# One core, a hybrid decoder layer: another pace of products in the issue order, the output projection's products in another order, the last branch's operands and the weight sums issued at other times

## The chip, the cores and the metric

The kernel runs on one core of one Trainium2 chip. The metric is the device time of one execution in microseconds. TensorE is called PE here, VectorE DVE, ScalarE ACT, GpSimd POOL and SyncE SP; each takes its instructions strictly in the order in which the program gives them, and waits for another engine or a transfer by semaphores.

## The reference, cut to what matters

One layer of a sequence model over 512 tokens of width 1024: two token mixers side by side, merged by gates, an output projection, and a gated feed-forward part.

```python
u = rmsnorm(h, g_mix[l])
proj = u @ w_in[l]          # retention q k v gate, DeltaNet q k v z, two merge gates
ro = retention_chunkwise(rotary(rq), rotary(rk), rv)           # 8 heads
y_ret = (silu(rgate) * groupnorm(ro)) @ w_ret_br[l]
qkv = silu(causal_dwconv(concat(dq, dk_, dv_), dn_conv_w[l]))
do = gated_delta_chunkwise(l2norm(cq), l2norm(ck), cv, g, beta)  # 8 heads, chunks of 128
y_dn = (rmsnorm(do) * silu(dz)) @ w_dn_br[l]
merged = sigmoid(gate_r) * y_ret + sigmoid(gate_d) * y_dn
h = h + merged @ w_o[l]
u2 = rmsnorm(h, g_ffn[l])
a, b = split(causal_dwconv(u2 @ w_up[l], ffn_conv_w[l]) + ffn_conv_b[l])
h = h + (silu(a) * b) @ w_down[l]
```

In each chunk of the DeltaNet a triangular system of 128 rows is solved for every head and chunk. All of it is float32.

## The kernel before

**Products.** Each float32 operand is split into a high and a low part, and one product of the layer becomes three on PE: high with high, high with low, low with high (`mm3`). A weight block is fetched by SP into `wraw` (L243, L245), cast on ACT to `whi`, and `wlo` is made on DVE as `wraw - whi`; both casts are issued some blocks ahead of their use, and SP fetches the next block when one has been split. All matmuls are recorded at L176, all transpositions at L180, and every instruction of ACT, DVE and POOL at L161, the line of a helper.

**Stages, in order of time.** Normalisation and transposition of x; input projections of the first four DeltaNet heads (`pk`, `pq`, `pv`, 256 or 512 columns); then the retention projections `pr`, while DVE solves the first four heads' triangular systems; the next four heads' and the gates' projections (`pz`) with the second solve; then five square matrices of 1024 x 1024, each by seven half-size products instead of eight: two merge gates (matrices 0 and 1), the DeltaNet branch (2), the retention branch (3, all as `py`), the output projection (4, called OUT, as `po`); then the feed-forward up projection (`pa`, `pb`) and down projection (`pd`, 5, called DOWN).

**A solve.** The kernel writes the matrices A to DRAM (L753), reads them back in another layout as `sa` (L816), and substitutes on DVE in 31 steps, each one `xtmp<-sa,xx` and one `xx<-xx,xtmp`. The result goes by DRAM (`x_dram`, L829) into `tt` (L832), SP issuing these transfers between its weight fetches. The small products `pm<-tt,A` on PE then combine the 32-row blocks; the first of them needs the whole solve.

**Seven products.** `PRODUCTS` (L61) names each product's weights and operand. Sums of weight quarters (`s1` to `s4`, table `SUMS`) are made in DRAM by POOL's DMAs (`presum`, L266): four copies and then four accumulating transfers of 1024 KB for each matrix, in pieces for DOWN. `presums` spreads them over a stretch of planned time; before each one ACT writes a small `tick` and POOL reads it into `tock`, so that the DMA is issued where ACT has come to. Matrix 3's sums are spawned with the eight `pz` blocks of the DeltaNet gate, OUT's after matrix 0, DOWN's after matrix 3. The operands of matrices 2 and 3 (`d` from the DeltaNet, `r` from retention; T1 to T4 are sums of quarters) are made by `operands_c`, chained one after another in `all_operands`, each part not before a given product (`since`) has begun; `oh` and `ol` are the two parts of such an operand.

**What sets the order.** The class `Order` (L102) is a planner that runs while the program is built. It has a clock, which every PE instruction advances (`product`, 512 columns by 512/2400 = 0.2133 us, from L173), and a clock for each other engine from a cost by size (DVE: 0.08 + 0.00104 us a column, so 0.61 us for 512 and 1.14 us for 1024; ACT: 0.12 + 0.00085; POOL: 0.3 + 0.001). Dependent work is written as generators, which are resumed when the planned clock has passed the planned end of their last instruction by 0.3 us (`HOP`) or more. So the planner's prices decide between which products a transposition or a small product stands, and in which order ACT, DVE and POOL take their work. Nothing of it runs on the chip.

**Output projection.** `m_out` transposes each finished quarter of the merged branches (`pmt`, copied to `mr`), and makes the operands: `mB` from quarters, `mt` and `mT` (T1 to T4) from their differences, each split on ACT and DVE. The products stand in the order 0, 3, 2, 5, 4, 1, 6 (`OUT_ORDER`) and are added into `h1` (x, loaded by SP at L1295 ahead of matrix 3) on DVE by `o_into`; when a row block is whole its sum of squares (`ssq`, by `junk`) gives `rs`, and `hs` is the scaled row, transposed on PE (`pt<-cst,hs`) and split to `u2hi`, `u2lo` for the feed-forward part.

## Time and profile before

| what | value |
|---|---|
| median of 3 runs | 1030.83 us (1028.68 to 1032.12) |
| profiled execution | 1029.81 us, its span 1028.0 us |
| PE busy | 993.4 us (97% of the span), 5241 instructions |
| DVE busy | 733.9 us (71%) |
| ACT busy | 528.7 us (51%) |
| POOL busy | 168.9 us (16%) |
| chain that ended last | PE 76%, DVE 14%, DMA 4%, issue 3%, ACT 2% |
| mean granted clock of PE | 0.985 |
| moved by DMA | 189.29 MB, mean 184 GB/s |

PE is busy nearly all the time, so a microsecond is to be had or lost mostly where PE stands idle, or where its clock is lowered. The share of the span does not show these places: the page's table of waits, the timeline and the table by stretches do. A wait is put down to the engine or transfer that came last.

### The profile page before, as it was taken

The page shows a single profiled execution, that of the slowest core. Times are in us where ns is not written, and L with a number is a line of the kernel's source. Part 1 is how long each engine was busy: PE and PEld are TensorE (multiplying, and loading weights), DVE is VectorE, ACT ScalarE, POOL GpSimd, SP SyncE. Part 2 cuts the span into 40 slices and gives each one's busy share as a digit, 9 for nine tenths or more (in the row PEclk, how much of TensorE's full clock was granted, in tenths as well). Part 3 has the DMA queues.
Part 4 walks back from the last instruction along what each step waited for, and adds up shares of the span by engine and source line. Part 5 has one row for each costly group of instructions (what it writes and reads, how often), then busy time and mean ns, then how long its engine had stood idle before and what let it go on. Part 6 is the DMA issues. An engine that isn't in the chain of part 4 may idle for free.

```text
span 1028.0 us, 14392 instructions
## 1 busy us (share of the span) xinstructions
PE 993.4 (97%) x5241; PEld 826.0 (80%) x5241; DVE 733.9 (71%) x1370; ACT 528.7 (51%) x1120; POOL 168.9 (16%) x220
## 2 busy tenths in 40 slices
PE   8999999999999998999999998899999999999997
PEld 7888887887788876888888776698888888888886
DVE  5777897457777785556789699856555676778785
ACT  5699222475545323557676456445444433346664
POOL 3021111023323112320111001221112111000001
PEclk9999999999999998999999989989999999999999
DMA  6343457856956935478889955835589899246763
GB/s 239 104 129 126 136 202 164 188 186 148 188 195 165 203 102 173 134 159 245 277 271 283 289 181 183 315 115 196 187 181 205 183 193 204 89 123 193 205 185 122
DMA packets 82614, 189.29 MB, mean 184 GB/s; under 512 B 23088, under 2 KB 31600, under 8 KB 82544
## 3 DMA queue, kind: packets, MB, share of 16 engines
q1 hardware_dynamic: 55024, 123.36, 36.9%
q0 software_dynamic: 27520, 65.02, 28.9%
q8 instruction: 41, 0.67, 0.3%
q14 instruction: 29, 0.24, 0.1%
HBM read 185.17 MB, written 68.19 MB: 246 GB/s over the span
## 4 chain that ended last, share of the span: by engine, by line
PE 76%; DVE 14%; DMA 4%; issue 3%; ACT 2%; POOL 1%; SPq 0%; POOLq 0%; DVEq 0%
PE py L176 14%; PE pa L176 12%; PE pb L176 12%; PE pd L176 10%; DVE wlo L161 4%; PE pq L176 4%; PE pk L176 3%; PE pz L176 3%; PE pv L176 3%; PE psc L176 3%; PE pr L176 3%; DVE xtmp L161 3%; PE po L176 2%; DVE xx L161 2%; PE pm L176 2%
## 5 line engine op out<-in xcount | busy, mean ns | idle before, releaser
L161 ACT CAST whi<-wraw 128x1024 fp32r<-128x1024 f32 x212 | 219.6, 1036 | 151.6 <-PE py L176 46.3
L161 DVE TENSOR_TENSOR wlo<-wraw,whi 128x1024 fp32r<-128x1024 f32 x212 | 254.7, 1203 | 52.9 <-ACT whi L161 52.5
L161 POOL TENSOR_SCALAR tock<-tick 128x1 f32<-128x1 f32 x72 | 27.8, 387 | 533.9 <-ACT tick L161 524.9
L161 DVE SCALAR_TENSOR_TENSOR acc<-pb,prm,acc 128x511 f32<-128x511 f32 (+1 forms) x44 | 33.0, 749 | 57.2 <-ACT acc L161 56.4
L176 PE MATMUL pa<-u2lo,whi 128*128 128x512 f32 (+1 forms) x192 | 72.4, 377 | 0.7 <-DVE u2lo L161 0.7
L176 PE MATMUL pa<-u2hi,whi 128*128 128x512 f32 (+1 forms) x192 | 72.7, 379 | 0.0
L176 PE MATMUL pa<-u2hi,wlo 128*128 128x512 f32 (+1 forms) x192 | 72.2, 376 | 0.0
L176 PE MATMUL pb<-u2hi,whi 128*128 128x512 f32 (+1 forms) x184 | 69.9, 380 | 0.0
L176 PE MATMUL pb<-u2lo,whi 128*128 128x512 f32 (+1 forms) x184 | 69.9, 380 | 0.0
L176 PE MATMUL pb<-u2hi,wlo 128*128 128x512 f32 (+1 forms) x184 | 69.9, 380 | 0.0
L176 PE MATMUL py<-whi,ol 128*128 128x512 f32 x160 | 63.3, 396 | 2.8 <-DVE ol L161 2.8
L176 PE MATMUL py<-whi,oh 128*128 128x512 f32 x160 | 63.6, 398 | 1.4 <-ACT oh L161 1.4
L176 PE MATMUL py<-wlo,oh 128*128 128x512 f32 x160 | 63.0, 394 | 0.0
L176 PE MATMUL pd<-whi,T 128*128 128x512 f32 (+1 forms) x198 | 55.4, 366 | 0.0
L176 PE MATMUL pz<-uhi,whi 128*128 128x512 f32 x128 | 53.0, 414 | 0.0
L176 PE MATMUL pr<-whi,uhi 128*128 128x512 f32 x128 | 52.5, 410 | 0.0
L176 PE MATMUL pz<-ulo,whi 128*128 128x512 f32 x128 | 50.6, 395 | 0.0
L176 PE MATMUL pz<-uhi,wlo 128*128 128x512 f32 x128 | 50.6, 395 | 0.0
L176 PE MATMUL pr<-whi,ulo 128*128 128x512 f32 x128 | 50.1, 391 | 0.0
L176 PE MATMUL pr<-wlo,uhi 128*128 128x512 f32 x128 | 50.0, 390 | 0.0
L161 DVE SCALAR_TENSOR_TENSOR acc<-pa,prm,acc 128x511 f32<-128x511 f32 (+1 forms) x44 | 32.9, 749 | 19.0 <-ACT acc L161 18.2
L176 PEld LDWEIGHTS pa<-u2lo,whi 128*128 128x128 f32 x192 | 37.1, 193 | 7.2 <-DVE u2lo L161 0.9
(320 smaller groups left out, 2456.1 us busy)
## 6 DMA issues: line engine op xcount, KB each, us to landing
wraw<-w SPq DMA_DIRECT2D x100, 512.0 KB, 4.6
s<-wm POOLq DMA_DIRECT2D x30, 1024.0 KB, 6.6
wraw<-s SPq DMA_DIRECT2D x60, 512.0 KB, 4.6
s<-wd POOLq DMA_DIRECT2D x24, 704.0 KB, 5.7
wraw<-wm SPq DMA_DIRECT2D x30, 512.0 KB, 4.8
s<-s POOLq DMA_DIRECT2D x10, 1024.0 KB, 11.3
wraw<-wd SPq DMA_DIRECT2D x15, 512.0 KB, 3.7
s<-s POOLq DMA_DIRECT2D x8, 704.0 KB, 8.9
```

The costliest lines, as they stand in the source:

```text
L161: return f(out, *args, **kw)
L176: self.engine.matmul(out, lhsT, rhs, start=start, stop=stop, **kw)
```

## The change

Five things change in the program; what is computed stays the same, up to the order of additions into `h1`.

1. In the planner each split float32 product costs 0.0135 us more: 0.2268 us for 512 columns instead of 0.2133, 0.1202 us for 256 instead of 0.1067. No other price is changed.
2. The output projection's products stand in the order 0, 5, 2, 3, 4, 1, 6. Product 5 is now alone in bank E; product 3 has a bank F of its own, which `fourth` adds to both halves of `h1`, so that DVE has two additions more. The banks are allocated where they are first used.
3. In `m_out`, B22 is split as soon as it is there; for B12, T2 comes first, T1 after 2.5 us and T3 after another 2.5 us of planned time, where T1 came first, then T2, B22 and T3.
4. The `r` operands are spawned on their own instead of behind the `d` operands, and their last parts may begin one product earlier (`since` 14, 15, 16, 17 for 14, 15, 17, 18).
5. The sums of matrix 3 and of OUT are issued one after the other, eight steps over 65 us of planned time each, from the `up` of the last DeltaNet head; matrix 3's no longer begin with the `pz` blocks, nor OUT's after matrix 0.

```diff
--- before.py
+++ after.py
@@ -57,7 +57,7 @@
 
 OUT, DOWN = 4, 5
 INNER = (HK, HK, HK, HK, HK, NK)
-OUT_ORDER = (0, 3, 2, 5, 4, 1, 6)
+OUT_ORDER = (0, 5, 2, 3, 4, 1, 6)
 PRODUCTS = (("w11", "B11"), ("w12", "B21"), ("s2", "T2"), ("s1", "T1"), ("s3", "T3"), ("s4", "B22"), ("w22", "T4"))
 WD = {"w11": 0, "w12": 1, "w21": 2, "w22": 3}
 SUMS = (("s1", "w21", "w22"), ("s3", "w11", "w21"), ("s2", "w11", "s1"), ("s4", "w12", "s2"))
@@ -170,7 +170,7 @@
     def matmul(self, out, lhsT, rhs, start, stop, **kw):
         m = max(lhsT.shape[-1], out.shape[-1])
         if lhsT.dtype == F32R:
-            self.order.product(max(256, out.shape[-1]) / 2400)
+            self.order.product(0.0135 + max(256, out.shape[-1]) / 2400)
         else:
             self.order.product(max(2 * m, 4 * out.shape[-1], 64) / 2400)
         self.engine.matmul(out, lhsT, rhs, start=start, stop=stop, **kw)
@@ -251,8 +251,11 @@
 
     def quarter(s, name):
         if name not in WD:
+            assert (s, name) in made
             return sums[s, name]
         return (io["wd"] if s == DOWN else io["wm"][s])[WD[name]]
+
+    made = set()
 
     def presum(s, parts):
 
@@ -265,6 +268,8 @@
                     kw = dict(accum_op=ALU.add) if add else {}
                     nc.gpsimd.dma_start(sums[s, name][:, c], quarter(s, b if add else a)[:, c],
                                         max_dma_last_dim=2048, **kw)
+                    if add and i == parts - 1:
+                        made.add((s, name))
                     yield
 
     def pace():
@@ -1159,21 +1164,24 @@
                 spawn(parts_of(opnd, (("B21", c), ("B22", c)), raw[c + HK]))
                 combine_c(raw, x, c)
                 yield gap
-        for c in range(HK):
-            while (x, c) not in sums_of or now[0] < since[2]:
-                yield 0.5
-            spawn(parts_of(opnd, (("T2", c), ("T4", c)), sums_of[x, c][1]))
-            yield gap
-        for c in range(HK):
-            while now[0] < since[3]:
-                yield 0.5
-            spawn(parts_of(opnd, (("T3", c), ("T1", c)), sums_of[x, c][0]))
-            yield gap
+        names = ("T3", "T1"), ("T2", "T4")
+        for n, i in enumerate((1, 0)):
+            for c in range(HK):
+                while (x, c) not in sums_of or now[0] < since[2 + n]:
+                    yield 0.5
+                spawn(parts_of(opnd, [(name, c) for name in names[i]], sums_of[x, c][i]))
+                yield gap
+
+    def late_sums():
+        while "up" not in heads[H - 1]["got"]:
+            yield 0.5
+        for s in (3, OUT):
+            yield from presums((s,), 1, (order.clock, order.clock + 65.0, 8))
 
     for src, raw, x in ((roT, rr_, "r"), (doT, dd, "d")):
         if x == "d":
             spawn(u_raw(), 8.0)
-            spawn(presums((3,), 1, (order.clock + 8.0, order.clock + 70.0, 8)))
+            spawn(late_sums())
         for c in range(8):
             spawn(gate_out(dense_c(u, "pz"), c, src, raw, x))
 
@@ -1181,9 +1189,9 @@
     def all_operands():
         yield from operands_c(u_opnd, None, "u", 1.2, (0, 0, 0, 0))
         yield from operands_c(d_opnd, dd, "d", 2.0, (8, 9, 12, 13))
-        yield from operands_c(r_opnd, rr_, "r", 2.0, (14, 15, 17, 18))
 
     spawn(all_operands())
+    spawn(operands_c(r_opnd, rr_, "r", 2.0, (14, 15, 16, 17)))
     gates = [{}, {}]
     merged = {}
 
@@ -1206,21 +1214,20 @@
         m = o_raw[name, half] = S(f"mr{t}{i}")
         act.copy(m, pt)
         yield
-        if name in ("B11", "B21"):
+        if name in ("B11", "B21", "B22"):
             spawn(o_split(name, half, m))
         if name == "B12":
-            t1 = S("mt1")
-            vec.tensor_tensor(t1, o_raw["B11", half], m, ALU.subtract)
-            spawn(o_split("T1", half, t1), 0.2)
-            yield
             t3 = S("mt3")
             vec.tensor_tensor(t3, o_raw["B22", half], m, ALU.subtract)
             t2 = o_raw["T2", half] = S("mt2")
             vec.scalar_tensor_tensor(t2, t3, -1.0, o_raw["B11", half], ALU.mult, ALU.subtract)
             spawn(o_split("T2", half, t2), 0.2)
-            yield 1.5
-            spawn(o_split("B22", half, o_raw["B22", half]), 0.2)
-            spawn(o_split("T3", half, t3), 1.8)
+            yield 2.5
+            t1 = S("mt1")
+            vec.tensor_tensor(t1, o_raw["B11", half], m, ALU.subtract)
+            spawn(o_split("T1", half, t1), 0.2)
+            yield 2.5
+            spawn(o_split("T3", half, t3), 0.2)
         elif name == "B21":
             yield 1.5
             t4 = S("mt4")
@@ -1285,7 +1292,6 @@
     hold(lambda: len(normed) == H and all("o" in hd["got"] for hd in heads))
     mix.close()
     late.append(ctx.enter_context(tc.tile_pool(name="heap2", bufs=1, reuse_waits="tile")))
-    spawn(presums((OUT,), 1, (order.clock, order.clock + 75.0, 8)))
     h1 = [[None] * 2 for _ in range(NT)]
     for s, opnd in ((1, u_opnd), (2, d_opnd), (3, r_opnd)):
         if s == 3:
@@ -1333,12 +1339,22 @@
         yield from split(u2hi[k][:, ck(t)], u2lo[k][:, ck(t)], ps, prm[:, P_GF + k:P_GF + k + 1])
         u2_ready.add((t, k))
 
-    A, E, C = ([PS("po") for _ in range(2)] for _ in range(3))
+    def fourth(t, ps):
+        yield from o_into(2 + t, 1, ps, ALU.subtract)
+        yield from o_into(2 + t, 0, ps, ALU.add, True)
+
+    def bank():
+        return [PS("po") for _ in range(2)]
+
+    A = bank()
     product(0, o_get, HK, [[(full, A[t], True, o_into(t, 0, A[t], ALU.add))] for t in range(2)])
-    product(3, o_get, HK, [[(full, E[t], True, o_into(2 + t, 1, E[t], ALU.subtract))] for t in range(2)])
+    E = bank()
+    product(5, o_get, HK, [[(full, E[t], True, o_into(2 + t, 0, E[t], ALU.add))] for t in range(2)])
     product(2, o_get, HK, [[(full, A[t], False, o_into(2 + t, 0, A[t], ALU.add))] for t in range(2)])
-    product(5, o_get, HK, [[(full, E[t], False, o_into(2 + t, 0, E[t], ALU.add, True))] for t in range(2)])
+    F = bank()
+    product(3, o_get, HK, [[(full, F[t], True, fourth(t, F[t]))] for t in range(2)])
     product(4, o_get, HK, [[(full, A[t], False, o_into(2 + t, 1, A[t], ALU.subtract, True))] for t in range(2)])
+    C = bank()
     product(1, o_get, HK, [[(full, C[t], True, o_into(t, 0, C[t], ALU.add, True))] for t in range(2)])
     product(6, o_get, HK, [[(full, A[t], False, o_into(t, 1, A[t], ALU.subtract, True))] for t in range(2)], tail=2)
     u2 = (u2hi, u2lo)
```

The counts of PE, ACT and POOL instructions stay as they are; DVE has two more. Where the instructions stand is another matter. Three places follow, first before and then now.

PE, at the first small product after the first solve (`tt` is the solve's result, `pr` the retention projections, whose `uhi_154` to `uhi_161` are the eight blocks of u):

```order
L176 MATMUL pr<-whi,ulo_163 128x512
L176 MATMUL pr<-whi,uhi_156 128x512
L176 MATMUL pr<-wlo,uhi_156 128x512
L176 MATMUL pr<-whi,ulo_164 128x512
L176 MATMUL pm_1907<-tt_178,A_632 32x32 x8
L176 MATMUL pr<-whi,uhi_157 128x512
L176 MATMUL pr<-wlo,uhi_157 128x512
```

```order
L176 MATMUL pr<-whi,uhi_161 128x512
L176 MATMUL pr<-wlo,uhi_161 128x512
L176 MATMUL pr<-whi,ulo_169 128x512
L176 MATMUL pm_1858<-tt_178,A_619 32x32 x8
L176 MATMUL pr<-whi,uhi_160 128x512
L176 MATMUL pr<-wlo,uhi_160 128x512
L176 MATMUL pr<-whi,ulo_168 128x512
```

Ahead of this `pm` stood 555 products of 512 columns and 96 of 256 columns; now 522 and 96 stand there. Thirty-three `pr` products have moved behind it. At the second solve the first `pm` has moved forward too, from 1146 products of 512 columns ahead of it to 1131.

ACT, at the last `tick` that releases one of OUT's sums on POOL (`oh<-r`, `oh<-rz`, `oh<-ry` are operands of matrix 3, `oh<-dz`, `oh<-dy`, `o<-r` of matrix 2 and 3, `res<-py` the copies of products):

```order
L161 CAST oh<-r_3978 128x512
L161 CAST whi<-wraw 128x1024
L161 COPY tick<-ones 128x1
L161 CAST whi<-wraw 128x1024
L161 CAST oh<-r_4039 128x512
L161 CAST whi<-wraw 128x1024 x2
L161 CAST oh<-rz_5691 128x512
L161 CAST whi<-wraw 128x1024
L161 CAST oh<-rz_5743 128x512
```

```order
L161 CAST oh<-dz_5401 128x512
L161 CAST whi<-wraw 128x1024
L161 COPY tick<-ones 128x1
L161 ACTIVATE res_5519<-py 128x512
L161 CAST oh<-dy_5273 128x512
L161 CAST whi<-wraw 128x1024
L161 ACTIVATE res_5538<-py 128x512
L161 CAST o<-r_3721 128x256
```

The last tick stood among the operands of matrix 3, thirteen rows ahead of the first `oh<-ry`; it now stands among those of matrix 2, thirty-six rows ahead of it.

DVE, at the first rows of the feed-forward part's input (`h_01`, `h_11` are the last halves of the first two row blocks, `hs` the scaled rows):

```order
L161 TENSOR_TENSOR h_01_5880<-h_01_5880,po 128x512
L161 SCALAR_TENSOR_TENSOR rs<-ssq_6293 128x1
L161 TENSOR_TENSOR h_11_5884<-h_11_5884,po 128x512
L161 TENSOR_TENSOR wlo<-wraw,whi 128x1024
L161 SCALAR_TENSOR_TENSOR rs<-ssq_6294 128x1
L161 TENSOR_TENSOR wlo<-wraw,whi 128x1024
L161 SCALAR_TENSOR_TENSOR junk,ssq_6291<-h_01_5880 128x512
L161 TENSOR_SCALAR hs<-h_20_5886,rr 128x512
L161 TENSOR_SCALAR hs<-h_21_5888,rr 128x512
```

```order
L161 SCALAR_TENSOR_TENSOR rs<-ssq_6302 128x1
L161 TENSOR_TENSOR h_01_5906<-h_01_5906,po 128x512
L161 SCALAR_TENSOR_TENSOR rs<-ssq_6303 128x1
L161 TENSOR_TENSOR h_11_5910<-h_11_5910,po 128x512
L161 TENSOR_TENSOR wlo<-wraw,whi 128x1024
L161 TENSOR_SCALAR hs<-h_20_5912,rr 128x512
L161 TENSOR_SCALAR hs<-h_21_5914,rr 128x512
L161 SCALAR_TENSOR_TENSOR junk,ssq_6300<-h_01_5906 128x512
L161 TENSOR_SCALAR hs<-h_30_5916,rr 128x512
```

Between the addition to `h_11` and the first `hs` stood two `wlo`, one `rs` and one `junk`; now one `wlo` stands there.

## The prediction

> **What bounds the kernel now.** I read the page's engine shares first, then the waits of PE, then the chain of waits, and then a table by stretches at the places that the waits name.
>
> ```profile
> PE 993.4 (97%) x5241; PEld 826.0 (80%) x5241; DVE 733.9 (71%) x1370; ACT 528.7 (51%) x1120; POOL 168.9 (16%) x220
> ...
> PE 76%; DVE 14%; DMA 4%; issue 3%; ACT 2%; POOL 1%; SPq 0%; POOLq 0%; DVEq 0%
> ```
>
> PE is busy for 97% of the span, and the same PE instructions are issued after the change. So only what PE loses can change: by standing still, or by running at a lowered clock. Yet a fifth of the chain that ended last is DVE, DMA and ACT: there are stretches in which PE has spare work in front of it only by the choice of the order. The table of PE's waits names them:
>
> ```profile
> PE pm L176 <- DMA tt<-x_dram: 6.2, 3, 4.3
> PE pt L180 <- DVE hs L161: 4.2, 1, 4.2
> PE py L176 <- DVE ol L161: 2.8, 2, 2.0
> ...
> PE po L176 <- DVE mT L161: 1.6, 1, 1.6
> PE po L176 <- ACT mT L161: 1.5, 1, 1.5
> PE py L176 <- ACT oh L161: 1.4, 1, 1.4
> ...
> PE po L176 <- DVE mB L161: 0.7, 1, 0.7
> ...
> PE pkt L180 <- ACT k L161: 0.3, 1, 0.3
> ```
>
> The columns are us in total, times, longest. Five places carry it: the first products after the two solves (6.2), matrix 3's first products (2.8 + 1.4 = 4.2), the output projection (1.6 + 1.5 + 0.7 = 3.8) and the first transposition of the feed-forward input (4.2). The table by stretches (columns: PE, PEld, DVE, ACT, POOL busy, then granted clock, DMA share, GB/s) shows who is full there:
>
> ```profile
> 111.00:166.00 55.00, 55.00 (x260) 45.54 (x259) 51.20 (x104) 12.77 (x19) 7.58 (x10) 1.00 0.54 170
> 342.00:380.00 38.00, 38.00 (x169) 31.45 (x169) 36.42 (x75) 10.75 (x16) 3.35 (x3) 1.00 0.60 154
> 580.00:590.00 10.00, 8.12 (x35) 6.16 (x33) 2.29 (x4) 2.60 (x5) 0.00 (x0) 1.00 0.98 375
> 590.00:600.00 10.00, 7.66 (x26) 5.94 (x27) 9.93 (x14) 6.66 (x11) 0.00 (x0) 0.66 0.51 159
> 630.00:640.00 10.00, 6.96 (x30) 5.11 (x29) 9.96 (x16) 8.19 (x14) 1.46 (x4) 1.00 0.56 183
> 640.00:650.00 10.00, 9.30 (x41) 7.38 (x40) 10.00 (x13) 3.97 (x6) 1.74 (x4) 1.00 0.92 306
> ```
>
> In the solves (first two rows) and in the output projection (last two) DVE has hardly a gap; at matrix 3 (580 to 590) the DMA engines are full, at 0.98.
>
> **The pace, and what it does at the solves.** PE's own pace, from the chain of waits (start, us, what):
>
> ```profile
> 166.98 6.00 DMA x_dram<-xx
> ...
> 379.71 3.56 DMA x_dram<-xx
> ...
> 384.61 4.58 DMA tt<-x_dram
> ...
> 389.87 3.97 PE pz L176 x9
> ...
> 593.30 3.78 PE py L176 x8
> ...
> 665.18 0.07 DVE rs L161
> 665.25 1.14 DVE wlo L161
> 666.38 0.61 DVE junk L161 x2
> ...
> 698.91 5.44 PE pa L176 x24
> ```
>
> 24 products of 512 columns take 5.44 us, 0.2267 each, so the new 0.2268 is right for PE and the old 0.2133 was 6% short. But the planner only weighs PE against its prices of the others, and those are short as well: it prices a `wlo` of 1024 columns on DVE at 0.08 + 1024 x 0.00104 = 1.14 us, where the timeline has 1.21; a solve's step of 31 columns at 0.08 + 0.03 = 0.11, where it has 0.21.
>
> ```profile
> 162.03 1.21 DVE L161 TENSOR_TENSOR wlo<-wraw,whi 128x1024 fp32r<-128x1024 f32 x1
> 166.44 0.21 DVE L161 TENSOR_TENSOR xtmp<-sa,xx 64x31 f32<-64x31 f32 x1
> 178.04 0.72 PE L176 MATMUL pm<-tt,A 32*32 32x32 f32 x16 [1.01 <-DMA tt<-x_dram]
> 387.99 0.31 PE L176 MATMUL pm<-tt,A 32*32 32x32 f32 x2 [4.29 <-DMA tt<-x_dram]
> ```
>
> A slower PE beside a DVE still priced too fast puts DVE's results too early between the products. At the first solve 33 products fewer stand ahead of the first `pm`: 33 x 0.2267 = 7.5 us. The solve's end doesn't follow. Its last step starts at 166.44, DVE having been busy for 51.20 of 55 us, and in DVE's new order only one `wlo`, 1.21 us, fewer stands ahead of that step; then come the write to DRAM (6.00) and the read back. So PE's wait of 1.01 becomes 1.0 + 7.5 - 1.2 = 7.3 us, a loss of **6.3**. After 4.29 us of idle time at the second solve nine products took 3.97 us instead of 9 x 0.2267 = 2.04: the granted clock was lowered there, at a price of 1.9. After 7.3 us I expect the same, so **+2.0** more, where the first solve so far had no such stretch. What is queued behind the `pm` is all of PE's work, `pr` products that were ready. Together +8.3, with bounds: 1.2 if the solve begins earlier too and the write is as short as at the second solve (worked out with the rivals), 11 if the clock stays low twice as long and the small products that follow wait once.
>
> The Trainium skill, TensorE: Matmul & The Clock Gate, section "Part 1: The HAM clock gate", says that PE's clock falls to half after about one idle window of 3.4 us and needs about as long a busy one to come back. The 4.29 us and the pitch after it agree; by the rule the low stretch costs half of 3.4, 1.7 us, where I take 2.0 from the row.
>
> At the second solve 15 products fewer stand ahead of the first `pm`, 3.4 us, while the number ahead of the A matrices (885) is unchanged, and again one `wlo` fewer is ahead of the solve's last step: 4.29 becomes 4.3 + 3.4 - 1.2 = 6.5, **+2.2**. The low clock is paid there already. One of matrix 3's sums, issued by POOL at the moment of these transfers, goes away, which could shorten the 4.58 us of `tt`; bounds -2 and +4.
>
> In the first head stages the transpositions of k stand up to 15 products (3.4 us) earlier. ACT's order has moved with them; the only wait there was 0.3 us (`pkt`). I take **+0.5**, bounds 0 and 3.
>
> **Matrix 3: the sums and the r operands.** The rows of SP, POOL and ACT before its first products:
>
> ```profile
> 569.64 1.27 POOL L266 DMA_DIRECT2D s<-s  x1 [4.87 <-issue]
> 571.28 5.97 SPq L1295 DMA_DIRECT2D h<-x  x8
> 579.09 10.97 SPq L243 DMA_DIRECT2D wraw<-s  x5
> 587.41 1.04 ACT L161 CAST whi<-wraw 128x1024 fp32r<-128x1024 f32 x1 [7.39 <-PE py L176]
> 594.32 0.63 PE L176 MATMUL py<-whi,oh 128*128 128x512 f32 x1
> 594.75 0.63 PE L176 MATMUL py<-whi,ol 128*128 128x512 f32 x1
> ```
>
> The page puts ACT's 7.39 us down to PE, but what came late is the weight block: SP issued eight loads of `h` and only then, at 579.09, the next fetches, and all of them ran against OUT's last accumulating sum (569.64). Behind the late cast in ACT's order stand the `oh<-ry` casts, and behind these PE's products: 4.2 us of waits, and then a lowered clock (594.32 and 594.75 lie 0.43 apart): 3.78 - 8 x 0.2267 = 1.97 for eight products and some 0.6 in the transpositions between, 6.8 in all. In the change the last sum stands 36 rows of ACT ahead of `oh<-ry` instead of 13, among matrix 2's operands, so its transfer is over before the loads of `h` start; and the r splits stand 8 rows earlier in ACT's order. A sum of 1024 KB reads two and writes one; at 375 GB/s these 3 MB are 8 us of what was in the way, more than the 7.39. I take **-6.8**; bounds -6.8 and 0 (below).
>
> **Output projection.** DVE is full there, so PE's waits go only as far as DVE's order brings the needed split forward; the work itself grows by two additions, 2 x 0.6.
>
> ```profile
> 639.85 0.60 DVE h L161
> ```
>
> T2 and B22 now come first, as products 5 and 2 need them; T1 and T3 are later, as 3 and 4 follow. At best the three waits are gone, -3.8; at worst the same work stands before the same end and grows by the additions, +1.2. The middle is -1.3; as DVE has no gap in either row (9.96 and 10.00 of 10), only the sequence within it can help, and I go nearer to the upper end: **-0.5**.
>
> **Feed-forward input.** Ahead of the first `hs` one `rs`, one `wlo` and one `junk` fall away, 0.07 + 1.14 + 0.61 = 1.8 us, so the wait of 4.2 becomes 2.4. But a `wlo` of 1.2 now stands between `hs` and the first `u2lo`, on which the first `pa` waits, so I count **-1.2**. The lowered clock stays: at matrix 3 idle times of at most 2.0 us were enough for it. By the skill's window of 3.4 us, cited above, a wait of 2.4 would not lower it, and the gain would be about 3.0.
>
> **The sum.** 0.5 + 8.3 + 2.2 - 6.8 - 0.5 - 1.2 = +2.5 us. The feed-forward part has the same order but for a few places, with FFN products at 0.2267 and no waits, and gets 0. From the profiled execution's 1029.81 us this makes **1032.3 us**; that execution was 1.0 us below the median of the runs, so the forecast is 1.5 us above it. A measurement of this kernel tells a change from none at about 0.3%, 3.1 us: the forecast lies inside that, as two large terms of opposite sign.
>
> **Rivals.**
>
> *A, the solves don't wait.* The first solve could start earlier: its last A matrix needs transpositions that now stand 12 products, 2.7 us, earlier. And the write to DRAM took 6.00 us there but 3.56 at the second solve, 2.4 less. Then the wait is 7.3 - 2.7 - 2.4 = 2.2, a loss of 1.2 without a lowered clock, 7.1 less than forecast. For it: the two rows of `x_dram`. Against it: DVE's order ahead of the A matrix is the same length as before. 1032.3 - 7.1 = 1025.2, and down to 1021 if the feed-forward clock stays up and the second solve gains.
>
> *B, matrix 3 still waits, slower.* The eight loads of `h` stay ahead of the fetch in SP's queue. If these 2 MB and the fetches fill the DMA engines by themselves, the block lands as late, `whi` and `oh` with it, and the 6.8 us don't come back: 1039.1 us. For it: SP's 5.97 us for these loads, and five fetches in 10.97 us. It decides if the first fetch behind the loads lands more than 6 us after its issue.
>
> *C, the sums come in the way elsewhere.* Sixteen steps now fall on matrices 0 to 2, one in 8 us, and an accumulating transfer takes long:
>
> ```profile
> s<-s POOLq DMA_DIRECT2D x10, 1024.0 KB, 11.3
> wraw<-s SPq DMA_DIRECT2D x60, 512.0 KB, 4.6
> ```
>
> If three fetches there come 1.5 us late each, that is +4.5: 1036.8. Against it: before, ten such transfers went by without a wait of `py` but the one at matrix 3.
>
> **How the numbers follow.** Forecast 0.40 (own range 1028 to 1037: 0.07 faster, 0.19 the same, 0.14 slower); A 0.34 (0.31 faster, 0.03 the same); B 0.17 (0.16 slower, 0.01 the same); C 0.09 (0.07 slower, 0.02 the same). Faster 0.38, the same 0.25, slower 0.37. The range is 1021 to 1041: A's low end, and B with a couple of us more at the first solve.
>
> **What would show it.** Right: a wait of `pm` on `tt` of 6 to 8 us at the first solve with a granted clock under 1 after it, and no `py` wait on `ol` or `oh` at matrix 3, with ACT's wait for `whi` there under 2 us. A is right if the first `pm` waits under 3 us; B if the `oh` and `ol` waits are still there; C if `py` waits at matrices 0 to 2. The forecast is wrong if PE's waits after the first solve add up to less than 4 us, or if a place that I gave nothing (the second half of the heads, the gates, the down projection) shows more than 3.

## The result, and the profile after

The changed kernel took **1041.95 us** (median of 4 runs, 1041.38 to 1042.65) against 1030.4 of the kernel before in the same sitting: 1.0112 times as long, 95% interval 1.0094 to 1.0131. It is slower. The forecast was 1032.3 us, inside a range up to 1041.0. The profiled execution has a span of 1040.5 us, 12.5 more than before. One run of the experiment "16.5 us instead of 9.0" below, 1127.05 us at a mean granted clock of 0.846, lies far outside the others of its kernel and is left out of its median.

The page of the changed kernel, the lines that answer to those shown of before:

```profile
PE 1001.7 (96%) x5241; PEld 826.6 (79%) x5241; DVE 738.8 (71%) x1372; ACT 529.0 (51%) x1120; POOL 171.5 (16%) x220
...
PE 56%; DVE 11%; issue 3%; DMA 1%; POOL 1%; SPq 1%; ACT 1%; POOLq 0%; DVEq 0%; ACTq 0%
```

The shares by engine on the chain are not to be compared here: this page's add up to 74%, so a good part of the chain could not be followed. The table of PE's waits of the changed kernel (us in total, times, longest) can be compared:

```profile
PE pm L176 <- DMA tt<-x_dram: 8.1, 3, 4.9
PE psc L176 <- DVE Sn L161: 4.4, 4, 2.5
PE pqt L180 <- ACT q L161: 3.7, 2, 2.3
PE pt L180 <- DVE hs L161: 2.3, 1, 2.3
PE pa L176 <- DVE u2lo L161: 2.0, 1, 2.0
...
PE pkt L180 <- ACT k L161: 1.7, 3, 0.8
PE po L176 <- DVE mT L161: 1.5, 1, 1.5
```

The waits of `py` on `oh` and `ol` are gone, that of `hs` has fallen from 4.2 to 2.3, as forecast. The wait on `tt` has grown, and two have come up that were not forecast: `pqt` on q, and more of `psc` on `Sn` (4.4 us for 1.8).

To see where the 12.5 us lie I lined the traces up by PE's work: at each product, its start less the time that all products ahead of it need at full pace (0.2267 us for 512 columns, and so on). This is the time that PE has lost so far, to waits and to a lowered clock. By stretches of the program (heads 0 to 3; the start of solve 0; its end and the first scans; the retention part and heads 4 to 7; solve 1 and its scans; matrices 0 to 3; output projection and feed-forward input), in us:

| stretch | before | changed | difference | forecast |
|---|---|---|---|---|
| heads 0 to 3 | 10.8 | 13.6 | +2.7 | +0.5 |
| start of solve 0 | 0.1 | 1.5 | +1.4 | 0 |
| end of solve 0, first scans | 6.5 | 18.3 | +11.8 | +8.3 |
| retention, heads 4 to 7 | 3.7 | 11.0 | +7.3 | 0 |
| solve 1 and its scans | 16.3 | 14.0 | -2.3 | +2.2 |
| matrices 0 to 3 | 7.7 | 1.0 | -6.6 | -6.8 |
| output projection, feed-forward input | 14.0 | 12.2 | -1.8 | -1.7 |

The back half came out at the forecast's size, -8.4 against -8.5. The error in the size is all in the front: +20.9 against +11.0. Each column rests on one trace, and single traces can differ by 2 or 3 us in how long the clock stays low behind a wait (shown at the end).

The table by stretches of the changed kernel (PE, PEld, DVE, ACT, POOL busy, granted clock, DMA share, GB/s) at solve 0 and at matrix 3's first products:

```profile
160.00:170.00 10.00, 10.00 (x46) 8.26 (x45) 5.80 (x15) 1.53 (x3) 2.42 (x2) 1.00 1.01 270
170.00:180.00 10.00, 3.94 (x19) 2.87 (x17) 3.14 (x6) 0.76 (x2) 1.50 (x2) 0.89 1.09 181
180.00:190.00 10.00, 8.64 (x64) 6.02 (x64) 5.13 (x12) 1.55 (x3) 0.00 (x0) 0.60 0.64 150
...
600.00:610.00 10.00, 9.42 (x46) 7.54 (x45) 6.77 (x9) 4.87 (x6) 0.00 (x0) 1.00 0.81 304
```

At solve 0 PE stands still for more than half of the ten us after 170 and then runs at a granted clock of 0.60, as forecast. But DVE has little to do there after 165.0, when it ends the solve (5.80 and 3.14 of 10); it is the DMA engines that are full, at 1.01 and 1.09. That was the first sign that the forecast had a nearly right size for a reason that was not the whole one.

### The profile page after: what moved, and what is told of

The parts are those of the page before. It is cut to its first block, busy times and chain, and to the rows that moved or that the text cites. A ratio compares the mean times of both kernels' runs of the same rounds, so it can differ in the third digit from the quotient of the medians.

```text
span 1040.5 us, 14401 instructions
## 1 busy us (share of the span) xinstructions
PE 1001.7 (96%) x5241; PEld 826.6 (79%) x5241; DVE 738.8 (71%) x1372; ACT 529.0 (51%) x1120; POOL 171.5 (16%) x220
## 4 chain that ended last, share of the span: by engine, by line
PE 56%; DVE 11%; issue 3%; DMA 1%; POOL 1%; SPq 1%; ACT 1%; POOLq 0%; DVEq 0%; ACTq 0%
PE py L176 12%; PE pb L176 12%; PE pa L176 12%; PE pd L176 10%; PE pz L176 3%; DVE wlo L161 2%; PE po L176 1%; DVE xtmp L161 1%; PE psc L176 1%; PE pro L176 1%; PE pk L176 1%; PE pv L176 1%; DVE xx L161 1%; DMA wraw<-s 1%; SPq L837 1%
## 5 line engine op out<-in xcount | busy, mean ns | idle before, releaser
L161 POOL TENSOR_SCALAR tock<-tick 128x1 f32<-128x1 f32 x72 | 32.3, 460 | 473.8 <-ACT tick L161 473.8
## 6 DMA issues: line engine op xcount, KB each, us to landing
s<-s POOLq DMA_DIRECT2D x10, 1024.0 KB, 10.8
```

What stands on the lines that cost most here:

```text
L161: return f(out, *args, **kw)
```

## The experiments

### One edit at a time

The change with the old pace, and the kernel before with the new pace alone:

```diff
-            self.order.product(0.0135 + max(256, out.shape[-1]) / 2400)
+            self.order.product(max(256, out.shape[-1]) / 2400)
```

> The change with the old pace (0.2133 us for 512 columns); the other four edits stay. Its front half has the issue order of the kernel before: 555 products of 512 columns ahead of the first small product after solve 0. Theory P (the pace alone makes the 21 us lost up to the scans of solve 1; the other edits alone make the 8.5 us won behind): 1030.4 - 8.5 = about 1022 us, wait of pm on tt back to some 6 us in all with 1.0 at solve 0, no waits of py on oh or ol. Rival Q (the gain at matrix 3 needs the new pace, or the moved sums cost in the front): about 1029 or more, py waits on ol and oh still there, or new waits before 440 us.

Measured: **1018.36 us**, 0.9881 times before (0.9863 to 0.9900). Without the pace the other four edits gain 12 us, more than the 8.5 expected. The trace doesn't show the whole of it: the profiled execution is the slowest of the four (1021.31 us), its span is 8.7 us shorter than before, and the other three took 1017.9 to 1018.8 us at a mean granted clock of 0.990 to 0.992 for its 0.987. In the trace solve 1 and its scans lose 14.2 us instead of 16.3, the heads some 0.9 more, and the output projection with the feed-forward input some 1 less, about half of what they won in the change.

> The kernel before with the new pace alone. Theory P: the front as in the change, +21 us by the end of the scans of solve 1, and the back as before: 1030.4 + 21 = about 1051 us, with the pm wait of about 7 us at solve 0 and py waits at matrix 3 of about 4 us. Rival Q: less than 1045 us, because part of the 21 us belongs to the moved sums (their transfers beside the solves), or because the pace alone brings matrix 3's gain.

Measured: 1045.08 us, 1.0142 times (1.0122 to 1.0162), +14.9. Up to the end of heads 4 to 7 its lost time is that of the changed kernel within 0.1 us (44.5 and 44.4), so the front's loss is the pace's and no other edit's. Then it gains at solve 1 and its scans (10.4 lost instead of 16.3), which the expectation of 1051 had not allowed for. Rival Q's figure (below 1045) was as near as Theory P's, but its reasons (the moved sums, matrix 3) are not what the trace shows: 6.9 us were still lost at the matrices.

The output projection's edits alone:

```diff
-OUT_ORDER = (0, 3, 2, 5, 4, 1, 6)
+OUT_ORDER = (0, 5, 2, 3, 4, 1, 6)
...
-        if name in ("B11", "B21"):
+        if name in ("B11", "B21", "B22"):
```

> The kernel before with the output projection's edits alone (order of products, own bank for product 3, splits in m_out). Theory P: only the part from the output projection to the first feed-forward products moves, by -0.9 (products) and -1.0 (hs, u2lo): 1028.5 us, waits of po on mT and mB of about 2 us instead of 3.8. Rival: the three waits go wholly, about 1026 us; or 1031 us and more, if the two more additions on DVE eat it.

Measured: 1028.13 us, 0.9976 times (0.9965 to 0.9987). The waits of `po` on `mT` are 2.2 us in all, as expected. The wait on `hs` did not fall, though, it is 4.9: the shorter way to `hs` comes with the new pace, not with these edits (in the change with the old pace it is 4.9 too, with the new one 2.3).

The moved sums and the r operands, together and one by one:

```diff
-            spawn(presums((3,), 1, (order.clock + 8.0, order.clock + 70.0, 8)))
+            spawn(late_sums())
...
-    spawn(presums((OUT,), 1, (order.clock, order.clock + 75.0, 8)))
...
-        yield from operands_c(r_opnd, rr_, "r", 2.0, (14, 15, 17, 18))
+    spawn(operands_c(r_opnd, rr_, "r", 2.0, (14, 15, 16, 17)))
```

> The kernel before with the moved sums and the r operands on their own, nothing else. Theory P: 4.2 us of py waits and 2.4 us of lowered clock at matrix 3 go, nothing else moves: 1030.4 - 6.6 = about 1023.8 us. At solve 1 the first of matrix 3's sums no longer runs beside the tt transfers, which may bring 0 to 1 us more. Rival B of the prediction (the h loads alone make the block late): within 2 us of before, oh and ol waits still there.

Measured: 1020.2 us, 0.9899 times (0.9875 to 0.9923). The matrices lose 1.1 us instead of 7.7, so the 6.6 came as expected; 3.0 come from solve 1 and its scans, beyond the 0 to 1 expected. (The profiled execution, 1017.81 us, won 2.3 more at the feed-forward input, with the same wait of 4.2 on `hs`: its clock was low there for a shorter time, which is shown at the end.)

> The kernel before with the moved sums alone; the r operands stay chained behind the d operands, with since 14, 15, 17, 18. Theory V (at matrix 3 the last sum's transfer was in the way of the weight block): the 6.6 us at matrix 3 go, and with the sum away from solve 1's tt about 2.5 us there: within 1 us of both edits together (1020.2). Rival W (the r splits, earlier in ACT's order, are what helps): py waits on oh and ol stay at 3 us or more, 1026 us and more.

> The kernel before with the r operands on their own alone (since 14, 15, 16, 17); the sums of matrix 3 and of OUT at their old times. Theory V: the weight block at matrix 3 is as late as before, the py waits stay at about 4 us, within 1 us of 1030.5. Rival W: about 1024 us, waits gone.

Measured: the sums alone 1022.21 us, 0.9922 (0.9897 to 0.9946); the r operands alone 1026.38 us, 0.9964 (0.9946 to 0.9981). At matrix 3 neither does it alone: of the 7.5 us lost there before, 4.7 and 6.4 remain, 0.9 with both. The row of the late cast on ACT, with the sums alone, and then the two latest rows with the r operands alone:

```profile
581.79 1.05 ACT L161 CAST whi<-wraw 128x1024 fp32r<-128x1024 f32 x1 [5.26 <-DMA wraw<-s]
582.75 0.61 ACT L161 CAST oh<-ry 128x512 fp32r<-128x512 f32 x1
```

```profile
582.33 0.61 ACT L161 CAST oh<-ry 128x512 fp32r<-128x512 f32 x1
589.59 1.04 ACT L161 CAST whi<-wraw 128x1024 fp32r<-128x1024 f32 x1 [6.64 <-DMA wraw<-s]
```

With the sums alone the block is there at 581.8 instead of 587.4 (3.3 us of this because the work ahead of it is done sooner), but all `oh<-ry` still stand behind it in ACT's order, and `py` waits 3.8 us on `ol`. With the r operands alone `oh<-ry` is done ahead of the block, but the block is later than ever (589.6); `py` no longer waits on `oh`, the wait has moved to `pmt` (3.7 us). So neither V nor W holds by itself: the block had to come earlier, and ACT's queue had to be emptied ahead of it.

What the sum's transfer did is seen at the loads of `h`. SP's rows of the kernel before, of the two kernels just told (the sums alone, then the r operands alone) and of the changed kernel:

```profile
571.28 5.97 SPq L1295 DMA_DIRECT2D h<-x  x8
```

```profile
569.84 4.00 SPq L1302 DMA_DIRECT2D h<-x  x8
```

```profile
573.86 7.81 SPq L1298 DMA_DIRECT2D h<-x  x8
```

```profile
593.53 4.00 SPq L1301 DMA_DIRECT2D h<-x  x8
```

With a sum issued 1.6 or 2.7 us ahead of them, SP takes 5.97 and 7.81 us to issue these loads, without one 4.00. From the first of them to the landing of the block behind them 16.0 us passed before and 15.7 with the r operands alone, 11.9 with the sums alone and 12.3 in the changed kernel. So the sum is worth some 4 us there. The fetch behind the loads is slow without it too: in the changed kernel, where the last sum had been issued 22 us ahead of the loads, it landed 8.2 us after its issue, as before, and ACT still waits for the block:

```profile
605.92 1.05 ACT L161 CAST whi<-wraw 128x1024 fp32r<-128x1024 f32 x1 [4.65 <-PE py L176]
```

(The page puts this down to PE, as it did before; the fetch, issued at 597.62, landed at 605.8.) PE doesn't wait, because the operands behind it were done by then.

### What makes the wait at solve 0

SP's and POOL's rows of the changed kernel at solve 0's way through DRAM (SP first, then POOL), and PE's rows behind it:

```profile
165.03 0.50 SPq L834 DMA_DIRECT2D x_dram<-xx  x1
...
169.08 15.70 SPq L837 DMA_DIRECT2D tt<-x_dram  x16
```

```profile
166.52 1.30 POOL L269 DMA_DIRECT2D s<-wm  x1
...
171.37 1.30 POOL L269 DMA_DIRECT2D s<-s  x1 [0.32 <-issue]
```

```profile
178.52 0.28 PE L176 MATMUL pm<-tt,A 32*32 32x32 f32 x2 [4.86 <-DMA tt<-x_dram]
181.36 0.63 PE L176 MATMUL pm<-tt,A 32*32 32x32 f32 x14 [2.56 <-DMA tt<-x_dram]
```

DVE ended the solve at 165.0, 1.9 us sooner than before, with PE 4.1 us later in its own work. SP then takes 15.70 us to issue the sixteen small loads of `tt`, from the first to the end of the last, where before it took 9.05. Two sums of 1024 KB were issued on this way, one beside the write and an accumulating one among the loads; before, one stood beside the write (167.01), and the accumulating one came at 178.14, when the first loads had landed. The sums stand at planned times, and the new pace had moved them against the solve.

Two runs on the changed kernel ask position against transfers. One gives the first `pm` its old place back, the other takes the two sums away and leaves the place:

```diff
-        yield 9.0
+        yield 9.0 if g else 16.5
```

> The change with one number more: the planner allows 16.5 us instead of 9.0 for the way of solve 0's result through DRAM, so that 555 products stand ahead of its first small product as before the change. Theory P (solve 0's loss of some 12 us beyond before, waits of 4.9 and 2.6 and the lowered clock, comes from that position alone): 11 to 12 us faster than the change, about 1030 us, pm wait under 2 us at solve 0. Rival: DVE or a transfer is late by itself there (the two sums beside it); then the wait stays above 3 us and less than 6 us are won.

Measured: 1035.05 us (nine runs, 1031.22 to 1042.81), 1.0057 times before (1.0030 to 1.0085). The first `pm` no longer waits, but the sixteen loads still take 16.19 us, and a wait of 5.0 us, of `pm` on a piece of `tt` that ACT copies, has come one step further on. Some 6 or 7 us are won, little more than half of what Theory P expected.

```diff
-                while order.clock < start + (end - start) * i / n:
+                late = {5: 16.0, 6: 13.0}.get(i, 0.0) if tuple(ss) == (0, 1, 2) else 0.0
+                while order.clock < start + (end - start) * i / n + late:
```

> The change with two of the early sums (issued at 166.5 and 171.4, beside x_dram and tt of solve 0) 16 and 13 us of planned time later. Nothing else of the order moves: 522 products still stand ahead of the first pm. Theory P: the position makes the wait, DVE's end and a round trip without company set it: of the 7.4 us of pm waits the second one (2.6) goes and the first shrinks by 1 to 2 us, 3 to 5 us faster: 1037 to 1039 us. Rival U (the transfers beside the solve make nearly all of it): 8 us and more faster, first wait under 1.5 us, no lowered clock.

Measured: 1034.1 us, 1.0036 times before (1.0021 to 1.0052), 7.9 us faster than the change. At the first `pm` the loss falls from 11.0 us to 0.4, though 33 products fewer still stand ahead of it:

```profile
165.23 0.49 SPq L835 DMA_DIRECT2D x_dram<-xx  x1
...
168.80 7.44 SPq L838 DMA_DIRECT2D tt<-x_dram  x16
```

```profile
173.75 0.44 PE L176 MATMUL pm<-tt,A 32*32 32x32 f32 x16
```

The loads take 7.44 us and PE doesn't wait. The ten us in which PE had stood still, in this kernel:

```profile
170.00:180.00 10.00, 10.00 (x89) 7.34 (x89) 8.01 (x17) 2.59 (x5) 1.76 (x2) 1.00 0.40 89
```

The DMA engines are at 0.40 there instead of 1.09, and the clock is not lowered. Rival U holds, though its 8 us came out at 7.9; my theory P, and with it the reason of the prediction's largest term, does not. Not all of it comes back: at the matrices this kernel loses 4.0 us where the change loses 1.0. ACT waits 6.0 us for the block behind the loads of `h`, and `pmt` 2.0 us on `res`:

```profile
597.89 1.05 ACT L161 CAST whi<-wraw 128x1024 fp32r<-128x1024 f32 x1 [6.02 <-DMA wraw<-s]
```

That a sum there is enough by itself is shown by the reverse: the old pace, the old place, and one accumulating sum moved in (the kernel it starts from, at 1015.6 us, is told below).

```diff
-                late = 4.0 if tuple(ss) == (0, 1, 2) and i == 21 else 0.0
+                late = {6: -5.0, 21: 4.0}.get(i, 0.0) if tuple(ss) == (0, 1, 2) else 0.0
```

> The former best, with one accumulating sum moved into solve 0's round trip as the new pace had moved it: the one issued at 177.5 5 us of planned time earlier, some 6 us after x_dram was issued, with the old pace and the old position of the first pm. Theory U: the sixteen tt transfers take about 15 us instead of 8.8, pm waits of 4 us and more and a lowered clock at solve 0, 5 to 11 us slower: 1021 to 1027 us, without any change of pace. Theory P (position): within 2 us of 1015.6.

Measured: 1020.11 us, 4.5 more than the 1015.6 of its start. The loads take 11.63 us:

```profile
172.80 11.63 SPq L838 DMA_DIRECT2D tt<-x_dram  x16
```

PE waits 1.4 and 2.1 us on what they bring, and then the clock is lowered:

```profile
180.00:185.00 5.00, 4.59 (x40) 3.27 (x41) 1.79 (x3) 0.01 (x1) 0.00 (x0) 0.66 0.71 116
```

The direction is U's, and so is the lowered clock; loads, waits and loss (11.63, 3.5 and 4.5 us) are a little below its figures (about 15, 4 and more, 5 to 11).

Is the place free, then? In the changed kernel PE comes 4.1 us late to solve 0, because it has waited in the heads, and DVE has not. So I moved the place in the best kernel, where PE is not late and no sum is near:

```diff
-        yield 9.0
+        yield 9.0 if g else 1.5
```

> The best kernel so far (old pace, three sums moved, 1013.3 us) with one number changed: the planner allows 1.5 us instead of 9.0 for solve 0's way through DRAM, so that 519 products instead of 555 stand ahead of its first small product, 8.2 us earlier, as in the change but with no sum beside the solve and no products late ahead of it. Theory X (the position costs what isn't taken up by PE being late itself: in the change PE was 4.1 us late before it, here it isn't): a pm wait of 5 to 7 us at solve 0 with a lowered clock behind it, 6 to 9 us slower: 1019 to 1022 us. Rival (DVE ends the solve earlier when less else stands ahead, the position is free): pm wait under 2 us, within 2 us of 1013.3.

Measured: 1023.72 us, 10.4 more than the 1013.3 of its start. PE's rows:

```profile
173.63 0.28 PE L176 MATMUL pm<-tt,A 32*32 32x32 f32 x2 [5.78 <-DMA tt<-x_dram]
174.68 0.63 PE L176 MATMUL pm<-tt,A 32*32 32x32 f32 x14 [0.77 <-DMA tt<-x_dram]
```

The wait is 6.6 us in all, as Theory X expected, and 10.2 us are lost with the lowered clock behind it, more than its 6 to 9. So the place costs what the prediction said, and more, when PE is in time. In the changed kernel 4.1 us of PE's lateness, the 1.9 us by which DVE was sooner and a shorter write had paid for it: from the issue of `x_dram` to that of the first load it took 4.05 us there and 3.57 with the two sums away, for 6.02 before. In the five kernels with the new pace and the old prices it is 3.6 to 4.1 us, in all with the old pace 5.5 to 6.3, with sums beside it or without; why is open.

### The sums elsewhere

Solve 1 won 2.3 us where I had forecast a loss. The time from issue to landing of the loads `sa` of both solves, before (min, median, max):

```profile
DMA to landing us min/median/max: 4.8/8.4/11.4
```

The longest are solve 1's two loads, 11.1 and 11.4, behind a sum that POOL issued at 329.60, 0.8 us ahead of them. In the changed kernel the sum stood 1 us behind them (355.30 against 354.35); the first load, which feeds the first sixteen steps, landed in 3.1 us, and the second, not needed before step 17, in 10.1. The 22nd sum moved later, on the change with the old pace:

```diff
-                while order.clock < start + (end - start) * i / n:
+                late = 4.0 if tuple(ss) == (0, 1, 2) and i == 21 else 0.0
+                while order.clock < start + (end - start) * i / n + late:
```

> The change with the old pace (1018.4 us) and one of the 24 early sums (the 22nd, issued on POOL at 330.44, 1 us ahead of the loads sa of solve 1) 4 us of planned time later. Theory T (that transfer, ahead of sa on the DMA engines, makes sa land in 11 us instead of 4.5, which is why solve 1 won in the change instead of losing): sa lands in 4 to 5 us, solve 1's wait on tt (2.8 us) goes, 3 to 6 us faster: 1012 to 1015 us. Rival: sa is slow because of the weight fetches; then 1018 us, sa still 10 us.

```profile
DMA to landing us min/median/max: 4.2/4.3/5.6
```

Measured: 1015.6 us, 2.8 us less than the 1018.36 of its start and 0.9857 times before (0.9842 to 0.9871), just short of the 3 to 6 expected. Theory T holds: one sum 4 us later, and solve 1's loads land in 4.2 us and the solve no longer waits for them.

```diff
-                late = 4.0 if tuple(ss) == (0, 1, 2) and i == 21 else 0.0
+                late = {5: 16.0, 6: 7.0, 21: 4.0}.get(i, 0.0) if tuple(ss) == (0, 1, 2) else 0.0
```

> The former best (the change with the old pace and the 22nd early sum later, 1015.6 us), with two sums more moved away: those issued at 166.4 and 177.5 beside x_dram and tt of solve 0, 16 and 7 us of planned time later. Theory U (transfers of the sums on the DMA engines set the round trip of a solve): the write to DRAM takes 3 to 4 us instead of 6, the wait of 1.1 at solve 0 goes, 0.5 to 1.5 us faster: about 1014.5 us. Rival: the two sums at 184 meet weight fetches and gb loads, and waits of psc or whi behind them take it back: 1016 us and more.

Measured: **1013.3 us**, 0.9839 times before (0.9810 to 0.9868), the best of all, though its runs (1011.97 to 1016.06) overlap those of the kernel that it starts from. The wait at solve 0 is gone (0.4 us lost there for 1.9), though the way of x_dram still takes 5.8 us.

The waits of `pqt` on q in the changed kernel have a sum behind them too. POOL's rows, then DVE's, ACT's and PE's:

```profile
343.91 1.30 POOL L269 DMA_DIRECT2D s<-s  x1 [0.35 <-issue]
344.71 1.58 POOL L161 TENSOR_TENSOR rk<-ssk,mhalf 128x4 f32<-128x4 f32 x1
```

```profile
346.33 0.17 DVE L161 TENSOR_TENSOR c<-beta,rk 128x4 f32<-128x4 f32 x1 [3.99 <-POOL rk L161]
...
347.84 2.31 DVE L161 SCALAR_TENSOR_TENSOR q<-pq,prm,q 128x511 f32<-128x511 f32 x3
```

```profile
350.24 0.63 ACT L161 ACTIVATE q<-q 128x512 f32<-128x512 f32 x1 [5.46 <-DVE q L161]
```

```profile
350.93 0.33 PE L180 MATMUL pqt<-cst,q 128*128 128x128 f32 x1 [2.25 <-ACT q L161]
```

A step `rk` of four columns stands on POOL behind a sum, which waits for its tick; DVE waits 3.99 us for it, with q's convolution behind it in DVE's order, and so on to PE. Not all of the 3.99 is the sum's: without it DVE waits 1.16 there, as the run below shows. Five sums moved in the changed kernel:

```diff
-                late = {5: 16.0, 6: 13.0}.get(i, 0.0) if tuple(ss) == (0, 1, 2) else 0.0
+                late = {5: 16.0, 6: 13.0, 13: 4.0, 22: -5.0, 23: 4.0}.get(i, 0.0) if tuple(ss) == (0, 1, 2) else 0.0
```

> The change, new pace included, with five of the 24 early sums at other times: the two beside solve 0's round trip as in the run before (1034.1 us), and three that POOL issued ahead of small steps or of solve 1's loads: the one at 246.9 (ahead of rgn and rk) 4 us of planned time later, the one at 333.4 (ahead of rk) 5 us earlier, the one at 345.2 (with sa) 4 us later. The issue order of PE, ACT and DVE stays that of the change but for the ticks. Theory U2 (most of what the pace cost came by the sums, which it moved to other places in the program): the two waits of pqt on q (3.7 us and a lowered clock) go, sa lands in 5 us instead of 10.6, 8 to 11 us faster than 1034.1: 1023 to 1026 us. Rival P2 (these waits come from the transpositions' own new positions): within 3 us of 1034, pqt waits still there.

Measured: 1028.6 us, 0.9985 times before (0.9963 to 1.0007). The waits of `pqt` are gone, and DVE waits for `rk` no longer than before the change:

```profile
330.44 0.16 DVE L161 TENSOR_TENSOR c<-beta,rk 128x4 f32<-128x4 f32 x1 [1.16 <-POOL rk L161]
```

The loss in the retention part and heads 4 to 7 is 4.1 us instead of 9.4 in the kernel with two sums moved. At solve 1 `sa` lands in at most 4.6 us, but nothing was won there (17.7 us lost against 16.6): with two sums moved, the first load had landed in 3.6 us already, and only the second, which has time, in 10.6. The matrices lose 4.5 us, with `pmt` waiting 2.5. So 5.5 of the 8 to 11 us came.

### The prices of DVE and ACT

```diff
-    vec = Engine(order, "vec", nc.vector, lambda n: 0.08 + 0.00104 * n)
-    act = Engine(order, "act", nc.scalar, lambda n: 0.12 + 0.00085 * n)
+    vec = Engine(order, "vec", nc.vector, lambda n: 0.12 + 0.00104 * n)
+    act = Engine(order, "act", nc.scalar, lambda n: 0.15 + 0.00085 * n)
```

> The change with DVE and ACT priced nearer to the trace too (0.12 + 0.00104 us a column for DVE, 0.15 + 0.00085 for ACT; a 1024-column wlo then 1.18 us where the trace has 1.21, a 31-column step 0.15 where it has 0.21). The first small product of solve 0 then has 552 products of 512 columns ahead of it (555 before, 522 in the change), that of solve 1 1146. Theory R (the loss comes from a right price for PE beside prices too low for the others): solve 0's pm wait under 2 us without a lowered clock, the q waits (3.7 us) mostly gone, 10 to 15 us faster than the change: 1027 to 1032 us. Rival S (any other order than the one the kernel was arranged with costs as much; the ratio of prices is not the point): waits of the same total turn up at other places of the front, 1037 us and more. The first k transposition stands 9 products earlier still, which is for S.

Measured: 1028.87 us, 0.9989 times before (0.9977 to 1.0002), 13.1 us faster than the change, in the range of Theory R. The reason is only partly R's. The first scans still waited (3.7 us of `pm` on `tt`, 2.9 on `ta`) and the way to the end of the scans lost 13.9 us where the change loses 18.3, and `pqt` waited 1.6. Its time comes down to that of before because solve 1 and its scans lose some 8 us instead of 16.3 and the matrices next to nothing. As this edit moves every sum as well, it cannot separate the ratio of prices from the place of the sums; that stays open.

## Why the prediction was wrong

**The whole.** The back half came within 0.1 us, in part by chance (matrix 3, below), but the time is 9.6 us past the forecast and just beyond the 1041 that the range allowed. The failed step is what the pace does in the front half: "A slower PE beside a DVE still priced too fast puts DVE's results too early between the products." That is one half of what a pace does. The planner's clock also sets when the 24 early sums are issued (those of matrices 0 to 2, spread from 110 to 325 us of planned time), and the prediction left them where they were. On top of the other four edits the pace costs 23.6 us (1041.95 against 1018.36). Moving five sums takes 13.4 us off (1028.6). That is not all a cost of the pace, as moving three sums gained 5.1 us with the old pace too: between the best times of either pace with sums moved, 1028.6 and 1013.3, 15.3 us remain. The traces put the largest part, some 8 us, at solve 1 and its scans, some 4 at the matrices, and some 4 in the work up to solve 0, the direct cost told below; what makes those at solve 1 is open.

The sign that the prediction named for being wrong did come: a place that it gave nothing, the second half of the heads, shows more than 3. Two of its three signs of being right came as well, the wait at the first solve and `py` without waits; the third, ACT waiting under 2 us for `whi` at matrix 3, did not (4.65).

**Solve 0, +8.3, measured +11.8.** The step "The solve's end doesn't follow" compared the shift of one place with DVE's work alone. It left out that PE would come late itself (4.1 us, DVE not), and it took the write and the read back as fixed, where the write became 2.0 us shorter and the two sums made the sixteen loads 15.7 us long. With the sums away the place cost 0.4 us. The total of the waits, 7.4 us, agrees with the forecast's 7.3 by chance. The lowered clock came, and cost more than the 2.0 taken: a dozen products 0.43 us apart where I had counted nine, and the small products between them.

**Retention and heads 4 to 7, 0, measured +7.3.** It was put at nothing, without a reason. 5.3 us went when two sums no longer stood ahead of POOL's small steps.

**Solve 1, +2.2, measured -2.3.** The first `pm` stood 15 products earlier, as said, but the first load of `sa` landed in 3.1 us instead of 11.1, because a sum now stood behind it instead of ahead, and the solve did not wait for it as it had before (4.1 us on DVE). The bound of -2 was set for another transfer.

**Heads 0 to 3, +0.5, measured +2.7.** Inside the bounds; `pkt` waited three times, 1.7 us instead of 0.3. With 1.4 more at the start of solve 0 (transpositions of the rotated k, `prkT`, waiting on DVE), it stays in both runs that keep the pace and move sums alone (13.8 and 14.0 us lost in the heads): a direct cost of the pace.

**Matrix 3, -6.8, measured -6.6.** The size was right, the reason only in part. The forecast put the last sum's transfer at 8 us of what made the block late; the runs show some 4 (16.0 to 12.3 us from the loads of `h` to the block's landing), and the fetch behind these loads lands 8.2 us after its issue with the sum or without it. The r operands had to be out of ACT's way as well: alone the two edits win 2.8 and 1.1 us at matrix 3, together 6.6. The late block is rival B's mechanism, and B's own sign (more than 6 us to landing) is there; only its cost stayed away, as PE had work in hand. With two and with five early sums moved `pmt` pays 2.0 and 2.5 us for it again.

**Output projection and feed-forward input, -1.7, measured -1.8.** `hs` waits 2.3 for a forecast 2.4, and `u2lo` 2.0; the shorter wait on `hs` is the pace's doing, as the output projection's edits alone leave it at 4.9. The clock was lowered there, as forecast: in the changed kernel's stretches, first by tens and then finer,

```profile
670.00:680.00 10.00, 7.69 (x37) 6.17 (x36) 8.61 (x19) 5.70 (x14) 2.94 (x6) 0.97 0.88 313
680.00:690.00 10.00, 8.04 (x42) 7.29 (x41) 8.56 (x29) 4.40 (x18) 3.27 (x6) 0.69 0.65 206
```

```profile
676.00:679.50 3.50, 1.19 (x7) 0.73 (x6) 2.65 (x5) 1.91 (x4) 0.10 (x1) 0.99 0.94 366
679.50:682.90 3.40, 3.40 (x16) 2.79 (x14) 3.40 (x9) 2.90 (x12) 0.00 (x0) 0.50 0.53 164
682.90:686.30 3.40, 1.44 (x12) 1.30 (x12) 3.40 (x15) 1.50 (x8) 1.88 (x5) 1.00 0.56 167
686.30:689.70 3.40, 3.40 (x19) 3.40 (x18) 2.26 (x7) 0.00 (x0) 1.39 (x2) 0.50 0.84 270
```

the granted clock is 0.69 from 680 to 690, in two low stretches of 3.4 us, one behind the wait of 2.3 us (to 679.1) and one behind that of 2.0 (to 685.0), with the full clock between them. The Trainium skill, TensorE: Matmul & The Clock Gate, section "Part 1: The HAM clock gate", names about one idle window of 3.4 us; by that the clock would have stayed up after a wait of 2.3. The trace does not agree here, as the forecast had assumed: one wait of 2.0 us was enough.

Each rival saw a part. A, that the solves would not wait, had solve 1 and the shorter write at solve 0; B had the late block at matrix 3, but not that PE would have work in hand; and C, that the sums would come in the way, had the mechanism, with the wrong sums and at the wrong place.

## What to carry to other kernels

A clock in a planner moves everything that is tied to it: before pricing a change of pace, list also the background transfers that are issued by that clock, and look at what each of them will stand beside and ahead of in its queue. A wait is the difference of two times, so losses at successive places don't add: what PE loses early is paid back at the next place where another engine, not held up itself, was the later one. And where a term comes out with the right size, take away its supposed cause before believing it.

## What the runs showed of the hardware

One background transfer of 1024 KB costs a chain of small transfers far more than its share: sixteen loads of 16 KB were issued in 7.4 us with no sum beside them, in 8.7 to 9.1 with one issued beside the write ahead of them, and in 11.6 and 15.7 when a second one came beside the loads. Two loads of 128 KB landed in 4.2 us each when the next sum was issued 1.7 us behind the second, both in 11 when one was issued 0.8 us ahead of them, and in 3.1 and 10.1 when one was issued 0.4 us behind the second. The order of issue alone doesn't settle it, though: in the best kernel the second load took 13.1 us with a sum 2.4 us behind it. And a transfer issued on POOL holds up what POOL computes: behind a sum that waited for its tick, `rk`, a step of four columns, made DVE wait 3.99 us, without it 1.16.

How long the clock stays low does not follow from the wait alone. The ten us from the first transposition of `hs`, in the kernel before and in the one with the sums moved and the r operands on their own; the order there is the same, and so is the wait ahead of it, 4.2 us:

```profile
667.50:677.50 10.00, 9.31 (x43) 8.69 (x44) 7.65 (x27) 4.33 (x17) 2.46 (x4) 0.53 0.46 148
```

```profile
657.80:667.80 10.00, 9.31 (x63) 8.45 (x64) 7.66 (x27) 4.32 (x17) 2.46 (x4) 0.83 0.45 148
```

The granted clock is 0.53 in one and 0.83 in the other, and PE begins 43 instructions in the one and 63 in the other. So a difference of 2 or 3 us behind a wait, between single traces, need not come from an edit.
